# Feed-forward up-projection of a transformer block: eight column pairs by seven block products instead of five, and the low halves of the down-projection's operands added by memory queues

## The chip, the cores and the metric

The kernel runs on one core of a Trainium2 chip. The metric is the device time of one execution in microseconds (us), as the median of several. The engines are named as the profile names them: PE (matrix products; PEld loads its stationary operand), DVE (elementwise on vectors), ACT (elementwise functions and copies), POOL (here it issues transfers and does little else) and SP (issues most transfers).

## The reference, cut to what matters

The kernel computes one layer on a sequence of 512 tokens with 1024 features: a normalisation, one input projection, two attention branches, an output projection with a residual, and then a gated feed-forward block with a causal convolution of width 3. The change lies in the feed-forward block:

```
D_MODEL = 1024; SEQ = 512; D_FF = 2816
def conv_glu(x, w_up, conv_w, conv_b, w_down):
    hid = x @ w_up                                   # 512 x 1024 by 1024 x 5632
    hid = conv_general_dilated(hid, conv_w, padding=((2, 0),), feature_group_count=2 * D_FF) + conv_b
    gate, up = hid[..., :D_FF], hid[..., D_FF:]
    return (silu(gate) * up) @ w_down                # 512 x 2816 by 2816 x 1024
...
x = x + conv_glu(rms_norm(x, norm2_g), w_ffn_up, ffn_conv_w, ffn_conv_b, w_ffn_down)
```

All of it is in float32.

## The kernel before

**Products in three parts.** PE multiplies operands that were rounded to a shorter float32 form. To keep accuracy, each operand is split in a high half (the rounded value, by ACT) and a low half (value minus high half, by DVE), and each product is three matmuls: high by high, high by low, low by high.

**The up-projection** (22 column pairs, up0 to up21) takes 128 columns of the gate half and the 128 matching columns of the up half at a time. A plain pair (`up_body`) is 48 matmuls of 512 tokens. A pair whose number stands in the table `SEVEN` (line 63: 5, 8, 11, 14, 17) is computed in `up_seven` (line 986) as a 2 x 2 by 2 x 2 block product with seven block products in place of eight; it is 84 matmuls of 256 tokens. For it, sums of the weight's blocks (`block_sums`, line 173, tile `sx`) and of the activations' blocks (`token_sums`, tiles `ts`) are formed first, and `up_seven` adds the seven products up into `hg` and `hu` with further DVE and ACT steps. After either kind, ACT and DVE do the convolution (`conv`: one ACT step, two DVE steps, for gate and for up) and the gate; the result stands in one of the four slots of `ub`.

**The operands of the down-projection.** After every second pair, `pair_sums` (line 870) takes the two new slots of `ub` as one column pair: four DVE sums into `st` (one buffer) and in place, and then high and low halves of the seven operands into two tiles, `ax` and `ay` (`halves`: a cast on ACT and a subtraction on DVE, four times). For the first seven column pairs `ay` is stored in memory (`ayd`) and fetched back later (`fetch`, line 948).

**The weights** come in chunks of 1 MB into the tile `raw` (two buffers; `load`, line 113, issued by SP). While PE works on one pair, the next pair's chunk is split into `whi` and `wlo` (two buffers each) by `split_gen`, or `split_seven` for a pair of seven products, with further tiles `wxh` and `wxl` (one buffer each) for the block sums. A chunk's load is issued when the chunk two before it has been split.

**The down-projection** (`down_body`, chunks dn0_0 to dn0_10 and dn1_0 to dn1_10) is another seven-product scheme, over `ax` first and over `ay` second.

**What sets the order.** Engines run their own instructions in order. Program order gives each instruction a priority (`run_chunk`, line 242, interleaves a pair's matmuls with the split of the next), and a scheduler lays out each engine's order from that. So the order on an engine may differ from the order of the source. In `BANK` (line 773) the eight accumulators are dealt out in turns.

## Time and profile before

| | us |
|---|---|
| median of 3 runs | 725.97 (725.83 to 726.38) |
| the profiled execution, its own time | 726.66 |
| its span, first to last instruction | 724.9 |
| PE busy | 718.6 (99% of the span) |
| DVE busy | 565.4 (78%) |
| ACT busy | 401.5 (55%) |
| POOL busy | 53.6 (7%) |

In a line of the timeline the first number is the start in us from the span's start, the second the duration. In a line of groups the numbers behind the bar are the busy time, the mean duration in ns, and the idle time before. The up-projection runs from about 403 to 616 us, the down-projection from 616 us to the end.

### The profile page before, as it was taken

The page shows a single profiled execution, that of the slowest core. Times are in us where ns is not written, and L with a number is a line of the kernel's source. Part 1 is how long each engine was busy: PE and PEld are TensorE (multiplying, and loading weights), DVE is VectorE, ACT ScalarE, POOL GpSimd, SP SyncE. Part 2 cuts the span into 40 slices and gives each one's busy share as a digit, 9 for nine tenths or more (in the row PEclk, how much of TensorE's full clock was granted, in tenths as well). Part 3 has the DMA queues.
Part 4 walks back from the last instruction along what each step waited for, and adds up shares of the span by engine and source line. Part 5 has one row for each costly group of instructions (what it writes and reads, how often), then busy time and mean ns, then how long its engine had stood idle before and what let it go on. Part 6 is the DMA issues. An engine that isn't in the chain of part 4 may idle for free.

```text
span 724.9 us, 10589 instructions
## 1 busy us (share of the span) xinstructions
PE 718.6 (99%) x4019; PEld 627.5 (87%) x4019; DVE 565.4 (78%) x1030; ACT 401.5 (55%) x727; POOL 53.6 (7%) x95
## 2 busy tenths in 40 slices
PE   8999999999999999999999999999999999999997
PEld 8999998888988888888889889889898988888886
DVE  6678867775988888566275799998979985997686
ACT  6675656657767676442254556655545653543541
POOL 2701200000101011000012000000000100000000
PEclk9999999999999999999999999999999999999999
DMA  8632232211313111314536613544335553564563
GB/s 308 250 131 78 83 117 74 74 59 58 118 63 113 59 59 59 136 68 144 195 149 239 203 62 156 186 135 160 118 145 186 181 184 117 173 243 174 177 222 116
DMA packets 24786, 100.91 MB, mean 139 GB/s; under 512 B 2592, under 2 KB 7328, under 8 KB 17184
## 3 DMA queue, kind: packets, MB, share of 16 engines
q1 hardware_dynamic: 21792, 87.00, 33.8%
q0 software_dynamic: 2656, 13.11, 5.0%
q8 instruction: 31, 0.51, 0.3%
q14 instruction: 19, 0.16, 0.1%
q10 hardware_dynamic: 288, 0.14, 0.1%
HBM read 88.44 MB, written 11.80 MB: 138 GB/s over the span
## 4 chain that ended last, share of the span: by engine, by line
PE 98%; DMA 1%; SPq 0%; DVE 0%; ACT 0%; DVEq 0%; issue 0%
PE P L1087 14%; PE p L998 7%; PE pg L254 4%; PE pg L253 4%; PE pg L255 4%; PE pu L254 4%; PE pu L255 4%; PE pu L253 4%; PE qkB L255 2%; PE gB L255 2%; PE qkB L253 2%; PE gA L253 2%; PE gA L254 2%; PE gB L253 2%; PE gA L255 2%; PE qkB L254 2%
## 5 line engine op out<-in xcount | busy, mean ns | idle before, releaser
L253 PE MATMUL pg<-hth,whi_up 128*128 128x512 f32 (+1 forms) x152 | 55.7, 367 | 0.0
L255 PE MATMUL pg<-hth,wlo_up 128*128 128x512 f32 (+1 forms) x152 | 55.7, 366 | 0.0
L254 PE MATMUL pg<-htl,whi_up 128*128 128x512 f32 (+1 forms) x152 | 55.7, 366 | 0.0
L254 PE MATMUL pu<-htl,whi_up 128*128 128x512 f32 (+1 forms) x152 | 55.6, 366 | 0.0
L253 PE MATMUL pu<-hth,whi_up 128*128 128x512 f32 (+1 forms) x152 | 55.6, 366 | 0.0
L255 PE MATMUL pu<-hth,wlo_up 128*128 128x512 f32 (+1 forms) x152 | 55.6, 365 | 0.0
L1087 PE MATMUL P<-whi_dn,ax 128*128 128x512 f32 x176 | 54.4, 389 | 0.0
L149 ACT CAST whi_dn<-raw_dn 128x1024 fp32r<-128x1024 f32 x33 | 34.3, 1051 | 25.5 <-PE P L1087 15.2
L145 DVE TENSOR_TENSOR wlo_dn<-raw_dn,whi_dn 128x1024 fp32r<-128x1024 f32 x33 | 40.0, 1224 | 9.2 <-ACT whi_dn L149 9.1
L228 DVE TENSOR_TENSOR wlo_up<-raw_up,whi_up 128x1024 fp32r<-128x1024 f32 (+1 forms) x40 | 41.2, 1062 | 7.0 <-ACT whi_up L226 7.0
L226 ACT CAST whi_up<-raw_up 128x1024 fp32r<-128x1024 f32 (+1 forms) x40 | 34.5, 917 | 14.7 <-PE pu L254 7.9
L1087 PE MATMUL P<-whi_dn,ay 128*128 128x512 f32 x132 | 40.8, 389 | 0.0
L1087 PEld LDWEIGHTS P<-whi_dn,ax 128*128 128x128 f32 x176 | 33.0, 188 | 6.8
L1087 PE MATMUL P<-wlo_dn,ax 128*128 128x512 f32 x88 | 34.2, 389 | 0.0
L254 PEld LDWEIGHTS pu<-htl,whi_up 128*128 128x128 f32 x152 | 28.6, 188 | 4.7
L253 PEld LDWEIGHTS pu<-hth,whi_up 128*128 128x128 f32 x152 | 28.5, 188 | 4.7
L255 PEld LDWEIGHTS pg<-hth,wlo_up 128*128 128x128 f32 x152 | 28.6, 188 | 4.7
L255 PEld LDWEIGHTS pu<-hth,wlo_up 128*128 128x128 f32 x152 | 28.5, 188 | 4.6
L253 PEld LDWEIGHTS pg<-hth,whi_up 128*128 128x128 f32 x152 | 28.6, 188 | 4.6
L254 PEld LDWEIGHTS pg<-htl,whi_up 128*128 128x128 f32 x152 | 28.6, 188 | 4.5
L633 DVE TENSOR_TENSOR_SCAN aB<-aB,reset 128x127 f32<-128x127 f32 (+3 forms) x32 | 26.0, 817 | 6.7 <-ACT aB L628 6.7
L1087 PEld LDWEIGHTS P<-whi_dn,ay 128*128 128x128 f32 x132 | 24.8, 188 | 5.1
(303 smaller groups left out, 2240.3 us busy)
## 6 DMA issues: line engine op xcount, KB each, us to landing
raw_up<-in_wts SPq DMA_DIRECT2D x22, 1024.0 KB, 4.8
raw_dn<-in_wd SPq DMA_DIRECT2D x11, 1024.0 KB, 4.8
raw_dn<-in_wd SPq DMA_DIRECT2D x11, 512.0 KB, 3.4
ayd<-ay POOLq DMA_DIRECT2D x7, 768.0 KB, 5.2
ay<-ayd POOLq DMA_DIRECT2D x7, 768.0 KB, 6.5
raw_gA<-in_wts SPq DMA_DIRECT2D x4, 1024.0 KB, 4.7
raw_qkB<-in_wts SPq DMA_DIRECT2D x4, 1024.0 KB, 4.8
raw_gB<-in_wts SPq DMA_DIRECT2D x4, 1024.0 KB, 4.7
```

What stands on the lines that cost most here:

```text
L145: chain("halves", V.tensor_tensor(o, x, y, op=op))
L149: chain("casts", A.copy(hi[:, sl], src))
L226: A.copy(hi[:, sl], raw[:, sl])
L228: E.tensor_tensor(lo[:, sl], raw[:, sl], hi[:, sl].bitcast(F32), op=ALU.subtract)
L253: PE.matmul(ps, sh, mh, start=first, stop=False)
L254: PE.matmul(ps, sh, ml, start=False, stop=False)
L255: PE.matmul(ps, sl, mh, start=False, stop=last)
L633: V.tensor_tensor_scan(ar, ar, reset[:, S - n:S - 1][:, ::-1], 1.0, op0=ALU.mult, op1=ALU.max)
L998: PE.matmul(ps, st, mv[:, k, :], start=first and k == 0 and n == 0, stop=last and k == 3 and n == 2, skip_group_check=True)
L1087: chain("products", PE.matmul(dst, st, mv, start=first and n == 0, stop=last and n == 2, skip_group_check=True))
```

## The change

The table `SEVEN` becomes 5, 8, 10, 12, 14, 16, 18, 20: eight pairs in place of five, from 8 on every second one. With it go these edits:

- `halves`, for the first nine column pairs: the low half is no longer subtracted on DVE. ACT writes the negated, rounded value into the low half (one more ACT step), and a transfer issued by POOL adds the unrounded value to it in place. The same form is used for the ninth column pair, which had tiles of its own.
- `up_fin`: a column pair's steps (sums, `ax`, `ay`, the store) go into a list `todo`, from which `run_chunk` takes one at each yield of the following pairs. `ay` has two buffers now (the two staging tiles), and its store comes a column pair later in the program.
- `ax0` is stored too (`axd`) and fetched back later into a slot of `ts`.
- `block_sums` and `split_seven`: the block sums are formed in place in `raw`, with one tile `s1` left of `sx`; the four sums and five low halves become four sums and five low halves of other sizes (the 1024-wide one of `sx` becomes two of 512).
- `pc` shrinks to one block; the copies of `up_seven` go into parts of `hg` and `hu` that are still free.
- The fetches of `ay` move: one after the last pair of seven, the others between the chunks of the down-projection.

The diff, cut to its core:

```diff
-SEVEN = (5, 8, 11, 14, 17)
+SEVEN = (5, 8, 10, 12, 14, 16, 18, 20)
...
     def block_sums(i):
-        sx = late["pool"].tile([P, 1536], F32, tag="sx", name=f"sx_{order[i]}")
+        s1 = late["s1"] = late["pool"].tile([P, S], F32, tag="s1", name=f"s1_{order[i]}")
         V.tensor_tensor(s1, b[:, 1], b[:, 3], op=ALU.add)
         yield
-        V.tensor_tensor(s2, s1, b[:, 0], op=ALU.subtract)
-        yield
-        V.tensor_tensor(s4, b[:, 2], s2, op=ALU.subtract)
-        yield
         V.tensor_tensor(b[:, 1], b[:, 0], b[:, 1], op=ALU.subtract)
...
+        part(hi, lo, 0, raw[:, 0:1024])
+        V.tensor_tensor(b[:, 0], s1, b[:, 0], op=ALU.subtract)
+        yield
+        part(wh, wl, 0, s1)
+        part(wh, wl, 512, b[:, 0])
+        yield
+        part(hi, lo, 1024, raw[:, 1024:2048])
+        V.tensor_tensor(b[:, 2], b[:, 2], b[:, 0], op=ALU.subtract)
+        yield
+        part(wh, wl, 1024, b[:, 2])
...
         for _ in body(*splits.pop(key)):
             next(sp, None)
+            if late.get("todo"):
+                late["todo"].pop(0)()
             yield
...
-                ins.append(V.tensor_tensor(a[:, n + o:n + sl.stop], src, a[:, sl].bitcast(F32), op=ALU.subtract))
+                if i < 9:
+                    A.activation(lo, src, AF.Copy, scale=-1.0)
+                    G.dma_start(lo, src, accum_op=ALU.add)
+                else:
+                    ins.append(V.tensor_tensor(lo, src, a[:, sl].bitcast(F32), op=ALU.subtract))
...
-            for step in pair_sums(j // 2):
-                step()
-            if j // 2 < 7:
-                G.dma_start(ayd[j // 2], pairs[j // 2][1].bitcast(F32))
+            i = j // 2
+            late["todo"] += pair_sums(i)
+            if 0 < i < 8:
+                late["todo"].append(lambda: G.dma_start(ayd[i - 1], pairs[i - 1][1].bitcast(F32)))
+            if i == 6:
+                late["todo"].append(lambda: G.dma_start(axd, pairs[0][0].bitcast(F32)))
...
-        if j == 18:
-            for i in range(5):
-                fetch(i)
+        if j == SEVEN[-1]:
+            keep[0] = fp.tile([P, S], F32, tag="hg", name="t2_0")
+            ax0 = fp.tile([P, 2048], F32R, tag="ts", name="ax0_", bufs=4)
+            G.dma_start(ax0, axd)
+            pairs[0] = (ax0, None)
+            fetch(0)
...
+            n = ({1: 1, 3: 5, 5: 6, 7: 2, 9: 3}, {0: 4})[s].get(i)
+            if n is not None:
+                fetch(n)
```

The order on the engines up to the split of up5 is the same in both kernels. Three places of the rest are shown. The first is PE in the middle of a pair of seven products; p1 and p6 are accumulators of that pair, pg that of the next plain pair's gate. Before, up11:

```order
L998 MATMUL p6_11_5268<-ts2_4565,wxh_up11_5208 128x256 x2
L998 MATMUL p6_11_5268<-ts2_4565,wxl_up11_5209 128x256
L998 MATMUL p1_11_5265<-hth_99,whi_up11_5206 128x256
L998 MATMUL p1_11_5265<-htl_100,whi_up11_5206 128x256
L998 MATMUL p1_11_5265<-hth_99,wlo_up11_5207 128x256
```

The same place in the changed kernel, in up10:

```order
L1008 MATMUL p6_10_5209<-ts2_4569,wxh_up10_5143 128x256 x2
L1008 MATMUL p6_10_5209<-ts2_4569,wxl_up10_5144 128x256
L258 MATMUL pg11_5344<-hth_99,whi_up11_5226 128x512
L259 MATMUL pg11_5344<-htl_100,whi_up11_5226 128x512
L1008 MATMUL p1_10_5206<-hth_99,whi_up10_5141 128x256
```

Two matmuls of the next pair, up11, now stand between the fourth and the fifth product of up10 (and two of up17 in up16); in the kernel before, seven of up18 stood so in up17.

The second place is DVE around the start of a chunk's block sums. In the kernel before, the low halves of a column pair's `ay` and `ax` (L909) stand among them:

```order
L228 TENSOR_TENSOR wlo_up10_5119<-raw_up10_4965,whi_up10_5118 128x1024
L183 TENSOR_TENSOR sx_up11_5155<-raw_up11_5026,sx_up11_5155 128x512
L1024 TENSOR_TENSOR hu8_4993<-hu8_4993,pc8_4991 128x256
L228 TENSOR_TENSOR wlo_up10_5119<-raw_up10_4965,whi_up10_5118 128x1024
L909 TENSOR_TENSOR ay3_4972<-ub_4184,ay3_4972 128x256
L899 TENSOR_TENSOR ub_4184<-ub_4184 128x256
L900 TENSOR_TENSOR st3_4973<-st3_4973,ub_4184 128x256
L853 SCALAR_TENSOR_TENSOR cg8_5081<-hg8_4992,par_88,cg8_5081 128x511
L200 TENSOR_TENSOR wxl_up11_5209<-sx_up11_5155,wxh_up11_5208 128x1024
L909 TENSOR_TENSOR ax3_4971<-st3_4973,ax3_4971 128x256
```

In the changed kernel, from the last step that reads up10's `raw` (the first row) to the first that reads up12's (`s1_up12`) and a little further:

```order
L195 TENSOR_TENSOR wxl_up10_5144<-raw_up10_4981,wxh_up10_5143 128x512
L859 SCALAR_TENSOR_TENSOR cg9_5164<-pg9_5127,par_88,cg9_5164 128x511
L860 SCALAR_TENSOR_TENSOR cg9_5164<-pg9_5127,par_88,cg9_5164 128x510
L231 TENSOR_TENSOR wlo_up11_5227<-raw_up11_5033,whi_up11_5226 128x1024 x2
L859 SCALAR_TENSOR_TENSOR ub_4185<-pu9_5128,par_88,ub_4185 128x511
L177 TENSOR_TENSOR s1_up12_5272<-raw_up12_5198 128x512
L860 SCALAR_TENSOR_TENSOR ub_4185<-pu9_5128,par_88,ub_4185 128x510
L1020 TENSOR_TENSOR pc10_5210<-hu10_5212,pc10_5210 128x256
```

The rows of low halves of `ay` and `ax` are gone. Between the last use of one `raw` and the first use of the next chunk in the same buffer stand five DVE steps (the two of `wlo_up11` share a row), and behind that first use stand the steps that read up9's last accumulator and those of up10.

The third place is ACT at a pair of seven products. Before, at up11 (`pc` takes the copies of p1, p5 and p7):

```order
L851 ACTIVATE ub_4184<-pu10_5193,par_88 128x512
L908 CAST ax4_5174<-st4_5176 128x256
L908 CAST ay4_5175<-ub_4184 128x256
L908 CAST ax4_5174<-ub_4184 128x768
L1003 COPY pc11_5269<-p1_11_5265 128x256
```

In the changed kernel, at up10:

```order
L229 CAST whi_up11_5226<-raw_up11_5033 128x1024 x2
L857 ACTIVATE ub_4185<-pu9_5128,par_88 128x512
L873 ACTIVATE cg9_5164<-cg9_5164 128x512
L1013 COPY hg10_5211<-p1_10_5206 128x256
L1016 COPY hu10_5212<-p5_10_5207 128x256
L1019 COPY pc10_5210<-p7_10_5208 128x256
L1026 COPY hg10_5211<-p1_10_5206 128x256
L910 CAST ay4_5205<-ub_4185 128x256
L913 ACTIVATE ay4_5205<-ub_4185 128x256
```

The column pair's casts stand behind the copies of the seven products now, each with a negated copy (L913) at its side, and the first copy of p1 stands behind the gate step of the plain pair (cg9).

More of the change, by code (lines that the diff above doesn't have):

```diff
@@ L175, in block_sums @@
         b = raws[i].rearrange("p (b c) -> p b c", c=512)
-        sx = late["pool"].tile([P, 1536], F32, tag="sx", name=f"sx_{order[i]}")
-        late["sx"] = sx
-        s1, s2, s4 = (sx[:, 512 * j:512 * (j + 1)] for j in range(3))
+        s1 = late["s1"] = late["pool"].tile([P, S], F32, tag="s1", name=f"s1_{order[i]}")
         V.tensor_tensor(s1, b[:, 1], b[:, 3], op=ALU.add)
-        yield
-        V.tensor_tensor(s2, s1, b[:, 0], op=ALU.subtract)
-        yield
-        V.tensor_tensor(s4, b[:, 2], s2, op=ALU.subtract)
         yield
@@ L193, in split_seven, with part @@
         splits[key] = tuple(t.rearrange("p (k c) -> p k c", c=P) for t in (hi, lo, wh, wl))
-        sx = late["sx"]
-        for j, (h, l, src) in enumerate(((hi[:, 0:1024], lo[:, 0:1024], raw[:, 0:1024]),
-                                         (wh[:, 0:1024], wl[:, 0:1024], sx[:, 0:1024]),
-                                         (hi[:, 1024:2048], lo[:, 1024:2048], raw[:, 1024:2048]),
-                                         (wh[:, 1024:1536], wl[:, 1024:1536], sx[:, 1024:1536]))):
-            A.copy(h, src)
-            V.tensor_tensor(l, src, h.bitcast(F32), op=ALU.subtract)
-            if j < 3:
-                yield
+        b = raw.rearrange("p (b c) -> p b c", c=512)
+        s1 = late["s1"]
+        def part(h, l, c0, src):
+            sl = slice(c0, c0 + src.shape[-1])
+            A.copy(h[:, sl], src)
+            V.tensor_tensor(l[:, sl], src, h[:, sl].bitcast(F32), op=ALU.subtract)
+        part(hi, lo, 0, raw[:, 0:1024])
[8 more added lines that the diff above has]
+        part(wh, wl, 1024, b[:, 2])
     def split_gen(i, pieces):
@@ L265, in block_kernel @@
     ayd = dram.tile([7, P, 1536], F32, tag="ayd", name="ayd")
+    axd = dram.tile([P, 2048], F32, tag="axd", name="axd")
     reset = pool_c.tile([P, S], F32, tag="reset", name="reset")
@@ L875, in pair_sums @@
         t = {}
-        if i < 8:
+        if i < 9:
             ax = fp.tile([P, 2048], F32R, tag="ax", name=f"ax{i}", bufs=8)
-            ay = fp.tile([P, 1536], F32R, tag="ay", name=f"ay{i}")
-        elif i == 8:
-            ax = fp.tile([P, 2048], F32R, tag="ts", name=f"ax{i}", bufs=4)
-            ay = fp.tile([P, 1600], F32R, tag="wxh", name=f"ay{i}")[:, 0:1536]
-            keep[0] = fp.tile([P, S], F32, tag="hg", name="t2_0")
+            ay = fp.tile([P, 1536], F32R, tag="ay", name=f"ay{i}", bufs=2)
         else:
@@ L907, in halves @@
                 sl = slice(o, o + src.shape[-1])
+                lo = a[:, n + o:n + sl.stop]
                 A.copy(a[:, sl], src)
-                ins.append(V.tensor_tensor(a[:, n + o:n + sl.stop], src, a[:, sl].bitcast(F32), op=ALU.subtract))
+                if i < 9:
+                    A.activation(lo, src, AF.Copy, scale=-1.0)
+                    G.dma_start(lo, src, accum_op=ALU.add)
+                else:
+                    ins.append(V.tensor_tensor(lo, src, a[:, sl].bitcast(F32), op=ALU.subtract))
             return ins
@@ L948, in fetch @@
     def fetch(i):
-        tag = {0: "sx", 1: "wxl"}.get(i, "ts" if i < 5 else "ax")
-        n, bufs = {"sx": (1536, 1), "wxl": (1600, 1), "ts": (2048, 4), "ax": (2048, 8)}[tag]
+        tag = {0: "wxl", 1: "wxh"}.get(i, "ts" if i < 5 else "ax")
+        n, bufs = {"wxl": (1600, 1), "wxh": (1600, 1), "ts": (2048, 4), "ax": (2048, 8)}[tag]
         ay = fp.tile([P, n], F32R, tag=tag, name=f"ay{i}", bufs=bufs)[:, 0:1536]
@@ L989, in body @@
             left, right = slice(0, 256), slice(256, 512)
-            pc = fp.tile([P, 3, 256], F32, tag="pc", name=f"pc{j}")
+            pc = fp.tile([P, 256], F32, tag="pc", name=f"pc{j}")
             hg = fp.tile([P, S], F32, tag="hg", name=f"hg{j}")
@@ L1002, in body @@
             prod(b1, r, 0, B(0, left), last=False)
-            A.copy(pc[:, 0], b1)
+            A.copy(hg[:, right], b1)
             yield
             prod(b5, w, 0, ts[1], last=False)
-            A.copy(pc[:, 1], b5)
+            A.copy(hu[:, left], b5)
             yield
             prod(b7, r, 1, ts[3], last=False)
-            A.copy(pc[:, 2], b7)
-            V.tensor_tensor(pc[:, 1], pc[:, 1], pc[:, 2], op=ALU.add)
+            A.copy(pc, b7)
+            V.tensor_tensor(pc, hu[:, left], pc, op=ALU.add)
             yield
             prod(b6, w, 1, ts[2])
-            V.tensor_tensor(hu[:, right], b6, pc[:, 0], op=ALU.add)
+            V.tensor_tensor(hu[:, right], b6, hg[:, right], op=ALU.add)
             yield
@@ L1023, in body @@
             V.tensor_tensor(hu[:, left], b7, hu[:, right], op=ALU.add)
-            V.tensor_tensor(hu[:, right], hu[:, right], pc[:, 1], op=ALU.add)
+            V.tensor_tensor(hu[:, right], hu[:, right], pc, op=ALU.add)
             up_fin(j, None, hu, g)
@@ L1050, in block_kernel @@
     late["ts"] = token_sums()
+    late["todo"] = []
     for j in range(NF):
@@ L1054, in block_kernel @@
             pass
-        if j == 18:
-            for i in range(5):
-                fetch(i)
+        if j == NF - 1:
+            for step in late["todo"]:
+                step()
+            late["todo"] = []
+        if j == SEVEN[-1]:
[4 more added lines that the diff above has]
+            fetch(0)
     BLK = {1: 0, 2: 1, 5: 2, 7: 3, 3: 0, 4: 1, 6: 2}
@@ L1174, in steps0 @@
             yield from late_pair(ss[i][:2])
-            fetch(i - 4)
     def steps1():
```

## The prediction

> **What bounds the kernel now.** I read the page first, for the share of each engine and the chain that ended last.

> ```profile
> span 724.9 us, 10589 instructions
> ...
> PE 718.6 (99%) x4019; PEld 627.5 (87%) x4019; DVE 565.4 (78%) x1030; ACT 401.5 (55%) x727; POOL 53.6 (7%) x95
> ...
> PE 98%; DMA 1%; SPq 0%; DVE 0%; ACT 0%; DVEq 0%; issue 0%
> ```

> PE holds 98% of the chain. A busy PE can still be a PE that is fed late, so the next view is what PE waited for in the whole span.

> ```profile
> PE warm L301 <- DVE warm L298: 1.1, 1, 1.1
> PE qA L379 <- ACT whi_qA L226: 0.6, 1, 0.6
> PE qA L379 <- DVE whi_qA L224: 0.4, 1, 0.4
> ```

> All three waits lie at the start of the kernel. In the up-projection PE never waits, so its time there is the sum of its matmuls, and only fewer or shorter matmuls make it shorter. The chain in order of time prices them: up6 starts at 445.49 us, the pair of seven products up8 at 467.28, up9 at 477.17.

> ```profile
> 445.49 0.23 PE pg L253
> ...
> 467.28 9.89 PE p L998 x84
> 477.17 0.23 PE pg L253
> ```

> Two plain pairs take 467.28 - 445.49 = 21.79 us, 10.895 each. A pair of seven products takes 9.89. The difference is 1.005 us a pair. What could spoil it is DVE, so I read the busy time of each engine (PE, PEld, DVE, ACT, POOL) over two stretches of three pairs each, one of seven products and two plain:

> ```profile
> 477.17:508.85 31.68, 31.68 (x182) 27.92 (x181) 29.43 (x48) 18.41 (x30) 1.07 (x2) 1.00 0.35 125
> 508.85:540.53 31.68, 31.68 (x182) 27.92 (x181) 26.00 (x40) 17.25 (x26) 0.53 (x1) 1.00 0.41 149
> ```

> DVE is busy 29.43 and 26.00 of 31.68 us, 87% on average, with PE at full clock (1.00).

> **The change part by part.**

> *PE.* Three more pairs become pairs of seven: 3 x 1.005 = 3.0 us less. The two matmuls of a later pair that move into up10 and up16 cost nothing by themselves. Everything else must be hidden behind PE, in periods of one plain pair and one of seven: 10.895 + 9.89 = 20.785 us.

> *DVE.* Durations in this trace overlap by the tail of each instruction, so I cost a step by the distance between starts of neighbours that did not wait.

> ```profile
> 476.74 0.69 DVE L928 TENSOR_TENSOR ub<-cg,ub 128x512 f32<-128x512 f32 x1
> 477.34 0.68 DVE L181 TENSOR_TENSOR sx_up<-sx_up,raw_up 128x512 f32<-128x512 f32 x1
> ...
> 481.28 1.22 DVE L228 TENSOR_TENSOR wlo_up<-raw_up,whi_up 128x1024 fp32r<-128x1024 f32 x1
> 482.41 0.42 DVE L909 TENSOR_TENSOR ay<-ub,ay 128x256 fp32r<-128x256 f32 x1
> 482.75 0.42 DVE L899 TENSOR_TENSOR ub<-ub 128x256 f32<-128x256 f32 x1
> ...
> 487.15 0.95 DVE L909 TENSOR_TENSOR ax<-ub,ax 128x768 fp32r<-128x768 f32 x1
> 488.02 0.75 DVE L854 SCALAR_TENSOR_TENSOR cg<-hg,par,cg 128x510 f32<-128x510 f32 x1
> 488.68 0.75 DVE L854 SCALAR_TENSOR_TENSOR ub<-hu,par,ub 128x510 f32<-128x510 f32 x1
> ```

> So 512 columns cost 0.60, 1024 cost 1.13, 256 cost 0.34, 768 cost 0.87, and a convolution step 0.66 us. Four low halves leave DVE per column pair: 0.87 + 0.34 + 0.34 + 0.60 = 2.15 us. What stays in a period of the changed kernel: four 1024-wide low halves of weights, 4.52; nine 512-wide steps (four block sums, three low halves, two gate products), 5.40; nine 256-wide ones (five in the pair of seven, four sums of the column pair), 3.06; eight convolution steps, 5.28. That is 18.26 of 20.785 us, 88%. The load per time is what it was: the low halves that leave pay for the pairs of seven that come closer together.

> *ACT* takes the negated copies.

> ```profile
> 477.09 2.00 ACT L226 CAST whi_up<-raw_up 128x1024 fp32r<-128x1024 f32 x2 [1.40 <-PE p L998]
> 478.99 0.40 ACT L908 CAST ay<-ub 128x256 fp32r<-128x256 f32 x1
> 479.30 0.82 ACT L851 ACTIVATE cg<-hg,par 128x512 f32<-128x512 f32 x1
> 480.02 1.03 ACT L199 CAST wxh_up<-sx_up 128x1024 fp32r<-128x1024 f32 x1
> ...
> 483.20 0.84 ACT L908 CAST ax<-ub 128x768 fp32r<-128x768 f32 x1 [0.60 <-DVE ub L899]
> ```

> The four casts of a column pair cost about 0.31 + 0.31 + 0.84 + 0.5 (512 columns, between the other two) = 2.0 us, and their negated copies as much again. By the windows ACT was busy 35.7 of 63.4 us, 56%; with 2.0 us and the denser pairs of seven I get about 70%. ACT has room.

> *Order within a period.* I laid the rows of the changed order out with these costs, from the start of a pair of seven such as up10 as time 0 (all of this is estimated from the rows above). At 0 PE has left up9, the buffer of `whi` is free, and ACT casts `whi_up11` until 2.0; DVE follows with `wlo_up11` until 3.4 and reaches `s1_up12` at 4.0. PE wants `whi_up11` at 4 x 12 x 0.1177 = 5.65 (9.89 us over 84 matmuls is 0.1177), because two matmuls of up11 stand there: 3.6 us in hand. The second accumulator of up9 is read by 5.2 and wanted after 9.89. The casts of up12 wait until PE has left up10; their first half is split by 14.5, and wanted at 20.785: 6.3 us in hand. The last step that reads up12's `raw` ends at 19.9; up14's load is issued then, and DVE wants it at 20.785 + 4.0 = 24.8. That leaves 4.9 us for a load:

> ```profile
> DMA to landing us min/median/max: 4.6/4.8/8.8
> ```

> Those are the loads of `raw_up`: 4.8 at the median just fits, and a late one delays `s1`. Behind `s1` on DVE stand the step that frees up9's second accumulator, and all steps of the pair of seven. A delay is not at once PE's: the first copy of p1 on ACT stands behind the gate step of the plain pair, which DVE feeds at 0.6, and PE writes p1 again at 5.65; DVE may be about 4.0 us late before PE waits. And DVE catches up as long as its loop is shorter than 20.785: from `s1` to the end of that chunk's last low half it has 14.0 us of work and 0.9 of waiting for ACT, then the load, then 0.2 for the handing over, 19.9 in all with 4.8. The loop breaks even at a load of 5.7 us.

> *Memory queues.* The trace of before shows no adding transfer. A column pair adds 1792 columns of 128 rows, 896 KB, in four transfers, issued by my layout from 8 to 13 us into the pair of seven. Three views bound them: the fetches at their busiest, then a load beside a store, then the stores and fetches by themselves.

> ```profile
> GB/s 195 66 186 213 252 326 405 441 423 354 177 9 0 0 0 0 0 159 239 425 310 0 20 86 246 412 425 425 430 405 396 418 403 427 399 47 13 9 133 337
> ...
> ay<-ayd POOLq DMA_DIRECT2D x5, 768.0 KB, 6.5
> raw_up<-in_wts SPq DMA_DIRECT2D x3, 1024.0 KB, 7.0
> ```

> ```profile
> raw_up<-in_wts SPq DMA_DIRECT2D x1, 1024.0 KB, 5.2
> ayd<-ay POOLq DMA_DIRECT2D x1, 768.0 KB, 5.4
> ```

> ```profile
> L933 POOL DMA_DIRECT2D ayd<-ay x7: 533/533/542, 438.8 to 553.9; - x7
> ...
> DMA to landing us min/median/max: 3.5/5.3/9.0
> ```

> At 425 GB/s the adds hold the queues for 2.2 us of a period; two loads hold them for 4.9 and the store for 1.9. Landing lies between 3.5 (the fastest store) and 18 us (twice the slowest, for a slow adder); I take 5.3, the median, since the pieces are smaller than the store. Adds that land by 18 and a store that lands by 24 lie beside the start of the load at 19.9; a load beside one store took 5.2. The adds' own results are wanted late: `st` is written again at 28, the `ub` slot at 35. POOL issues five transfers of 0.53 us a period and has nothing else to do, so their cost there is nothing; without that cover it would be 2.7 us a period.

> [...]

> *The way into the down-projection.* `ax0` returns by POOL as soon as PE has left the second product of up20, some 18 us before PE wants it; the fetches beside it took up to 9.0. Its cost is nothing; if it came at twice 9.0, nothing still. The other fetches, moved into the down-projection, are wanted a whole first pass later (264 matmuls of 0.23, some 60 us).

> *The sum.* The profiled execution took 726.66 us, 1.8 more than its span and 0.7 more than the median. Less 3.0 it is 723.6, and against the median 725.97 - 3.0 = 723.0.

> **The rivals.**

> *Loads too slow for the loop (slower).* If the loads of `raw` reach 7.0 us beside the adds and the store, as three did beside the fetches, the loop is 22.1 us, 1.3 over the period. Five loops from up10 to up20 lose 6.5, of which 4.0 are hidden: 2.5 us, a net of 725.5. Up to 6.8 the loss stays at 5 x 1.1 - 4.0 = 1.5 and within the forecast's side. From 7.4 us on the kernel is slower than before by over 1.45: 5 x 1.7 - 4.0 = 4.5 lost against 3.0 won. At 8.8, the slowest seen, 5 x 3.1 - 4.0 = 11.5, and the time is 734.5. For it speaks that the load just fits; against it, that a load beside one store took 5.2 and that the adds fall between the loads. PE would wait for ACT's copy of p1, or for `whi`.

> *The adds themselves too slow (slower).* `st` has one buffer; the next column pair's sums wait for the adds, and DVE stands behind them. From those sums to the last add's issue are 5.7 us, so the loop is 5.7 plus the landing, and breaks even at a landing of 15. At 18 it is 23.7, 2.9 over; seven more column pairs lose 20.4, less 4.0 hidden: 16.4, and the time is 739.4. The nearest rows (3.5 to 9.0) speak against it.

> *The change gains half.* A single slow load now and then, or the down-projection's first chunk late by a microsecond or two, costs 1.6 to 4.4 us once: 724.6 to 727.4.

> **How the numbers follow.** A measurement of this kernel can tell about 0.2%, 1.45 us, from no change. The forecast has 0.62: every term that must be hidden has a margin by the rows, except the load. The middle case has 0.13, loads over 7.4 have 0.18, and slow adds have 0.07. So faster is 0.62, the same 0.13, slower 0.25. At the low end nothing can give more than the three pairs; with the spread of the runs, 0.5 us, that is 722.4. At the high end the range takes in the middle case and loads up to 7.7 us (5 x 2.0 - 4.0 = 6.0 lost), 729.0; what it leaves out is 0.17.

> **What would show it.** Right: the pairs of seven at 9.89 us and the plain ones at 10.9, up21 ending 3.0 us earlier, no wait of PE in the up-projection, DVE at about 88% there, loads of `raw_up` at about 5. The first rival would show as waits of DVE's `s1` step for `raw_up`, and of PE for ACT's copies into `hg` or for `whi`; the second as waits for `st` or `ub` on a transfer from POOL. The prediction is wrong if PE waits between up8 and dn0_0 for more than 1.5 us in sum, or if the plain pairs stretch without a wait in the trace.

## The result, and the profile after

The changed kernel takes 732.97 us (median of 4 runs, 731.74 to 734.34), the kernel before 725.90 (4 runs, 725.54 to 726.38): a ratio of 1.0097, 95% interval 1.0084 to 1.0109. It is slower by 7.1 us; the forecast was 3.0 faster. The profiled execution took 733.51 us with a span of 731.5, 6.6 more than the span before.

The page of the changed kernel: span, engines, the queue that POOL feeds (packets, MB, share of 16 engines), and the chain that ended last.

```profile
span 731.5 us, 11010 instructions
...
PE 718.2 (98%) x4127; PEld 629.9 (86%) x4127; DVE 567.3 (78%) x1035; ACT 426.7 (58%) x789; POOL 86.3 (12%) x133
...
q0 software_dynamic: 8128, 23.47, 12.3%
...
PE 82%; DVE 5%; DMA 5%; issue 4%; ACT 2%; POOL 1%; SPq 0%; DVEq 0%; POOLq 0%; ACTq 0%
```

PE's share of the chain fell from 98% to 82%; DVE, the memory queues and POOL, which held 1% of it or less, hold 5, 5 and 1% now. PE's busy time didn't change (718.2 us, 718.6 before), although three more pairs are of the kind that is 1.0 us shorter: part of it is matmuls at a lower clock (0.84 in the mean of the 11 us around the stop in up8, below). What PE waited for, over the whole span (us in total, times, longest):

```profile
PE p L1008 <- ACT hg L1013: 2.9, 1, 2.9
PE qA L385 <- ACT whi_qA L229: 2.4, 1, 2.4
PE P L1105 <- DVE wlo_dn L145: 1.2, 2, 0.8
...
PE p L1008 <- DVE wlo_up L195: 0.8, 1, 0.8
PE p L1008 <- ACT whi_up L194: 0.4, 1, 0.4
```

Three waits on L1008, 4.1 us, are all in one pair of seven products; two on L1105 are in the first pass of the down-projection; that on `qA` is at the start of the kernel. Three pieces of the chain in order of time show that one pair (start, length) beside others:

```profile
478.09 5.97 PE p L1008 x36
...
501.09 4.09 PE p L1008 x36
515.63 9.89 PE p L1008 x84
```

The second part of up8, 36 matmuls, took 5.97 us where the same 36 of up10 took 4.09. PE had stood still for 2.90 us ahead of it and ran at a mean clock of 0.84 in these 11 us (clock, share of the DMA engines and GB/s are the last three columns):

```profile
474.00:485.00 11.00, 8.10 (x51) 7.73 (x51) 10.44 (x19) 7.47 (x15) 2.83 (x4) 0.84 0.92 277
```

From the first matmul of up5 to the first of up9 it is 47.9 us (436.0 to 483.9), before 41.6: 6.3 us lost in up8, of which 4.1 are waits and 5.97 - 4.09 = 1.9 the lower clock (0.50 granted from 478.92 to 482.12 us). The rest, 0.3, is by estimate the overlap of neighbouring matmuls that each stop breaks (rows of 0.28 us start 0.11 apart). From up9 to the first matmul of `P` it is 135.4 us, before 138.6: the 3.2 us that the forecast hoped for. From the first to the last matmul of `P` it is 107.5 us, before 104.7: 2.8 lost. The start of the kernel came 0.6 later. Together 0.6 + 6.3 - 3.2 + 2.8 = 6.5 of the 6.6 us.

**Why up8 stalls.** DVE ahead of it waits 6.61 us for a transfer before it may write `st`:

```profile
457.32 0.69 DVE L935 TENSOR_TENSOR ub<-cg,ub 128x512 f32<-128x512 f32 x1
464.62 0.42 DVE L899 TENSOR_TENSOR st<-ub 128x256 f32<-128x256 f32 x1 [6.61 <-DMA ay<-st]
```

That transfer is the last add of the column pair before. POOL's rows at that place (in brackets: how long POOL did nothing, and what it is put down to):

```profile
444.49 0.56 POOL L940 DMA_DIRECT2D ayd<-ay  x1 [6.51 <-DVE st L899]
449.00 0.89 POOL L914 DMA_DIRECT2D ay<-ub  x1 [3.95 <-DVE hu L1034]
452.44 0.86 POOL L914 DMA_DIRECT2D ax<-st  x1 [2.55 <-ACT ub L857]
455.44 0.84 POOL L914 DMA_DIRECT2D ax<-ub  x1 [2.15 <-DVE ub L859]
461.22 0.86 POOL L914 DMA_DIRECT2D ay<-st  x1 [4.93 <-issue]
```

The four adds (L914) don't go out together. They land 3.1, 2.7, 5.5 and 3.3 us after their issue, at 452.1, 455.1, 460.9 and 464.5, and each of the other three starts 0.3 us after the landing of the one above, whatever DVE or ACT row the trace puts the gap down to. The first of them went out 0.3 us after the store of `ax0` had landed (at 448.7), 5.1 us behind the sums. So 15.5 us pass from the first issue to the last landing, while `st` of the next column pair is wanted at 458.0.

**The way into the down-projection.** The chain holds two loads of `raw_dn` there:

```profile
619.52 8.66 DMA raw_dn<-in_wd
...
638.49 7.14 DMA raw_dn<-in_wd
```

The landing (min/median/max) of all 22 loads of `raw_dn` in the kernel before:

```profile
DMA to landing us min/median/max: 3.0/4.4/4.9
```

The same in the changed kernel:

```profile
DMA to landing us min/median/max: 3.2/4.3/10.3
```

The slow ones were issued between 602 and 644 us, when `ax0` and five fetches of `ay` came back (POOL issued them from 601.88 to 616.28; they took 6.2 to 11.7 us), and then the last two fetches (636.73 and 642.60).

### The profile page after: what moved, and what is told of

It reads as the page before. It is cut to its first block, busy times and chain, and to the rows that moved or that the text cites. A ratio compares the mean times of both kernels' runs of the same rounds, so it can differ in the third digit from the quotient of the medians.

```text
span 731.5 us, 11010 instructions
## 1 busy us (share of the span) xinstructions
PE 718.2 (98%) x4127; PEld 629.9 (86%) x4127; DVE 567.3 (78%) x1035; ACT 426.7 (58%) x789; POOL 86.3 (12%) x133
## 4 chain that ended last, share of the span: by engine, by line
PE 82%; DVE 5%; DMA 5%; issue 4%; ACT 2%; POOL 1%; SPq 0%; DVEq 0%; POOLq 0%; ACTq 0%
PE P L1105 10%; PE p L1008 9%; DMA raw_dn<-in_wd 2%; PE pg L258 2%; PE pu L258 2%; PE pg L260 2%; PE pg L259 2%; PE pu L259 2%; PE pu L260 2%; PE qkB L260 2%; PE gB L260 2%; PE qkB L258 2%; PE gA L259 2%; PE gB L258 2%; PE gA L258 2%
## 5 line engine op out<-in xcount | busy, mean ns | idle before, releaser
L1105 PE MATMUL P<-whi_dn,ax 128*128 128x512 f32 x160 | 49.5, 390 | 0.0
L258 PE MATMUL pg<-hth,whi_up 128*128 128x512 f32 (+1 forms) x128 | 46.4, 363 | 0.0
L260 PE MATMUL pg<-hth,wlo_up 128*128 128x512 f32 (+1 forms) x128 | 46.4, 362 | 0.0
L259 PE MATMUL pg<-htl,whi_up 128*128 128x512 f32 (+1 forms) x128 | 46.3, 362 | 0.0
L259 PE MATMUL pu<-htl,whi_up 128*128 128x512 f32 (+1 forms) x128 | 46.3, 362 | 0.0
L258 PE MATMUL pu<-hth,whi_up 128*128 128x512 f32 (+1 forms) x128 | 46.3, 362 | 0.0
L260 PE MATMUL pu<-hth,wlo_up 128*128 128x512 f32 (+1 forms) x128 | 46.2, 361 | 0.0
L1105 PE MATMUL P<-whi_dn,ay 128*128 128x512 f32 x132 | 40.8, 389 | 0.0
L231 DVE TENSOR_TENSOR wlo_up<-raw_up,whi_up 128x1024 fp32r<-128x1024 f32 (+1 forms) x34 | 33.6, 1032 | 5.6 <-ACT whi_up L229 5.4
L229 ACT CAST whi_up<-raw_up 128x1024 fp32r<-128x1024 f32 (+1 forms) x34 | 28.5, 894 | 12.8 <-PE pu L259 9.1
L1105 PEld LDWEIGHTS P<-whi_dn,ax 128*128 128x128 f32 x160 | 30.0, 188 | 6.1
L1105 PE MATMUL P<-wlo_dn,ax 128*128 128x512 f32 x80 | 31.7, 396 | 1.5 <-DVE wlo_dn L145 1.2
L641 POOL TENSOR_SCALAR_AFFINE_SELECT bB<-bB 128x128 f32<-128x128 f32 x32 | 13.7, 430 | 149.1 <-DVE bB L640 139.5
L1105 PEld LDWEIGHTS P<-whi_dn,ay 128*128 128x128 f32 x132 | 24.8, 188 | 5.1
L670 ACT CAST pth_A<-pT_A 128x128 fp32r<-128x128 f32 (+2 forms) x40 | 14.7, 371 | 22.4 <-PE pT_A L657 14.7
## 6 DMA issues: line engine op xcount, KB each, us to landing
raw_up<-in_wts SPq DMA_DIRECT2D x22, 1024.0 KB, 5.7
raw_dn<-in_wd SPq DMA_DIRECT2D x11, 1024.0 KB, 5.8
ayd<-ay POOLq DMA_DIRECT2D x7, 768.0 KB, 5.7
ay<-ayd POOLq DMA_DIRECT2D x7, 768.0 KB, 9.1
raw_gA<-in_wts SPq DMA_DIRECT2D x4, 1024.0 KB, 4.8
raw_qkB<-in_wts SPq DMA_DIRECT2D x4, 1024.0 KB, 4.8
raw_gB<-in_wts SPq DMA_DIRECT2D x4, 1024.0 KB, 4.8
```

The costliest lines, as they stand in the source:

```text
L229: A.copy(hi[:, sl], raw[:, sl])
L231: E.tensor_tensor(lo[:, sl], raw[:, sl], hi[:, sl].bitcast(F32), op=ALU.subtract)
L258: PE.matmul(ps, sh, mh, start=first, stop=False)
L259: PE.matmul(ps, sh, ml, start=False, stop=False)
L260: PE.matmul(ps, sl, mh, start=False, stop=last)
L641: G.affine_select(b[:, n - P:n], b[:, n - P:n], pattern=[[-1, P]], compare_op=ALU.is_gt, fill=0.0, base=0, channel_multiplier=1)
```

## The experiments

The theories, as the expectations number them. First: what sends the adds out one after the other is the room that transfers issued by POOL are given (`dynamic_dma_scratch_size`, 512 bytes in both kernels). The expectations take it for memory that holds descriptors; the runs show it only by how many transfers are on their way. Its rivals: something that more room wouldn't mend, such as the adds' own speed and traffic (2); the store of `ax0` that stands among the adds in POOL's queue (3). Fourth, for the down-projection's part: the fetches that moved there slow its loads. The kernel before took 726.06 to 726.22 us beside these runs.

### More room

```diff
-    nc = bacc.Bacc("TRN2", target_bir_lowering=False, num_devices=1, dynamic_dma_scratch_size=512)
+    nc = bacc.Bacc("TRN2", target_bir_lowering=False, num_devices=1, dynamic_dma_scratch_size=1024)
```

> The changed kernel with twice the memory for descriptors of POOL's transfers (1024 bytes a partition in place of 512); the order on every engine is the same. Theory 1 (descriptor room): an add fills so much of that room that POOL can't issue the next before the last has landed; with twice the room the adds of a column pair go out about 0.9 us apart, the last lands some 8 us earlier, the 6.6 us wait of the sums step for the adds is gone and with it PE's loss of 6.4 us in up8: 733.0 - 6.4 = 726.6 us. Theory 2 (the adds themselves are slow, in the queues): the adds issue earlier but each lands later, the last one lands when it did, up8 still loses about 6 us: 732 to 734 us. Both leave the 2.8 us that are lost at the start of the down-projection.

Measured: 724.89 us (10 runs, 724.64 to 726.73), ratio 0.9990 (0.9981 to 0.9999), 8.1 us less than the change with the same instructions in the same order on every engine. POOL's rows for the adds of the column pair ahead of up8:

```profile
458.20 0.84 POOL L914 DMA_DIRECT2D ay<-ub  x1 [3.68 <-DVE ub L900]
459.48 0.87 POOL L914 DMA_DIRECT2D ax<-st  x1 [0.44 <-DVE cg L859]
460.95 0.86 POOL L914 DMA_DIRECT2D ax<-ub  x1 [0.59 <-ACT ax L913]
464.58 0.84 POOL L914 DMA_DIRECT2D ay<-st  x1 [2.76 <-ACT ay L913]
```

All that PE waited for in this kernel, at its start:

```profile
PE qA L385 <- ACT whi_qA L229: 1.3, 1, 1.3
PE warm L307 <- DVE warm L304: 1.1, 1, 1.1
```

The first three adds went out before the first landed (at 461.7, 3.5 us after its issue), and the last landed 9.7 us after the first issue. Three is the most here: of the column pair before, the fourth add went out at 450.04, 0.3 us after the first had landed, with the second and third still on their way. The landing (min/median/max) of all adds in the changed kernel:

```profile
DMA to landing us min/median/max: 2.6/3.9/7.3
```

And with 1024 bytes, where it is nearly the same, so that it is not the speed of one add that made the difference:

```profile
DMA to landing us min/median/max: 2.6/3.5/6.5
```

DVE waits for no add, PE for nothing in the up-projection; up5 to up9 takes 41.6 us as before the change. The first theory holds, and the second falls.

### Room between the two

The same line with 768 in place of 1024.

> The changed kernel with 768 bytes for POOL's descriptors. If 512 bytes hold three plain transfers, an add counts as two of them, and the room grows with the bytes, 768 hold four: two adds are on their way at a time, and only the third waits for the first to land. A column pair's four adds then end some 5 us sooner than with 512 bytes, the wait of 6.6 us for st falls under 2 us and PE's loss in up8 goes; the fetches at the way into the down-projection go out four at a time: 725 to 728 us. Rival: the room comes in coarser steps (768 works as 512): adds one after the other as in the change, 731 to 734 us.

Measured: 725.17 us (10 runs, 724.43 to 726.92), ratio 0.9991 (0.9981 to 1.0001). POOL's rows for one column pair:

```profile
443.02 0.86 POOL L914 DMA_DIRECT2D ay<-ub  x1 [5.76 <-DVE hu L1023]
443.69 1.07 POOL L914 DMA_DIRECT2D ax<-st  x1
450.09 0.84 POOL L914 DMA_DIRECT2D ax<-ub  x1 [5.33 <-ACT cg L857]
450.77 1.03 POOL L914 DMA_DIRECT2D ay<-st  x1
```

Two adds go out at once; the third follows 0.3 us after the first has landed (449.8), the fourth 0.3 after the second (450.5). So the number of adds on their way is 1, 2 and 3 with 512, 768 and 1024 bytes, and two are enough: PE waits for nothing in the up-projection here, and 0.4 us at the down-projection. Of plain transfers five were on their way at the fetches, one more than expected, and the sixth went out 0.3 us after the first had landed; with 512 bytes it is three, as the kernel before had shown already, in rows that I hadn't read this way (the three of the first row land from 578.0 on):

```profile
572.82 1.61 POOL L953 DMA_DIRECT2D ay<-ayd  x3 [18.37 <-PE p L998]
578.29 0.54 POOL L953 DMA_DIRECT2D ay<-ayd  x1 [3.86 <-PE pg L255]
```

### The store moved behind the adds

```diff
-                    G.dma_start(lo, src, accum_op=ALU.add)
+                    late["add"] = (G.dma_start(lo, src, accum_op=ALU.add),)
...
-                late["todo"].append(lambda: G.dma_start(axd, pairs[0][0].bitcast(F32)))
+                late["todo"].append(lambda: behind(G.dma_start(axd, pairs[0][0].bitcast(F32)), late["add"]))
```

> The changed kernel with the store of the first column pair's ax moved from right behind its adds to behind the adds of the seventh column pair. Theory 3 (place of this store): it holds the descriptor room and the queues from 437 to 449 us, so that the second column pair's adds start 5 us late; without it they end some 5 to 7 us earlier, the sums step waits 0 to 2 us instead of 6.6, and the time is 726.6 to 728 us. Theory 1 in its strict form (adds one after the other are enough to lose the time) gives 731 to 733: the four adds of a column pair still take 15 us.

Measured: 731.68 us (4 runs, 729.62 to 735.05), ratio 1.0081 (1.0052 to 1.0110). The adds of the second column pair still went out from 447.4 to 463 us, one after the other, and DVE waited for them at five places:

```profile
DVE st L899 <- DMA ay<-st: 16.6, 5, 7.5
```

The four started 1.1 us behind their sums in place of 5.1, as theory 3 had it, but the last landed 20.2 us behind them, 20.6 in the change: the landings themselves took longer (5.2, 2.6, 7.1 and 3.2 us), and they still stand in a row. Theory 3 falls as the cause; what the store's place is worth, at most the 1.3 us between the medians, is inside the spread of these four runs.

### The fetches issued by SP

```diff
-                SP.dma_start(raw, wd0[n])
+                late["ld"] = (SP.dma_start(raw, wd0[n]),)
...
-        G.dma_start(ay, ayd[i])
+        if i == 0:
+            G.dma_start(ay, ayd[i])
+        else:
+            behind(SP.dma_start(ay.bitcast(F32), ayd[i]), late["ld"])
```

> The changed kernel with six of the seven fetches of ay issued by SP, each behind a weight load of the down-projection, in place of POOL just after the last pair of seven. Theory 4 (the fetches slow the weight loads): raw_dn loads land in 5 to 6 us, in place of up to 10, PE does not wait at the start of the down-projection, 2.8 us come back: 730.2 us. Rival (DVE comes late out of the up-projection, and the loads only look late): PE still waits for the split of dn0 chunks, 732 to 734 us. The loss in up8 stays with both.

Measured: 731.61 us (730.78 to 732.62), ratio 1.0072 (1.0055 to 1.0088). All of PE's waits behind the start:

```profile
PE p L1011 <- ACT whi_up L194: 1.9, 1, 1.9
...
PE p L1011 <- ACT hg L1016: 1.5, 1, 1.5
PE p L1011 <- DVE wlo_up L195: 0.8, 1, 0.8
```

The waits on L1105 are gone and the down-projection's matmuls take 104.8 us again, 2.7 less than in the change; the loss in up8 (L1011 here) stays. That is the fourth theory by the trace. The medians are 1.4 us apart, but four runs each overlap (731.74 to 734.34 in the change), so they alone don't show it. The loads didn't come down to the 5 to 6 us that were expected: some of `raw_dn` still take up to 9.3, but none of them is late for PE.

### The low halves on DVE

```diff
-                if i < 9:
+                if i < 0:
```

All eight pairs of seven, no add: every low half is subtracted on DVE again.

> Eight pairs of seven products, but all low halves subtracted on DVE as before, no adds by transfers. By the ledger DVE has 18.3 + 2.15 = 20.4 us of work in a period of 20.8 us. If DVE is then the bound (theory 5: the adds are needed), DVE falls behind by its waits for ACT and for loads, about 1 us a period, and PE loses 2 to 6 us by up20: 725 to 730 us. If the slack of the buffers is enough (rival: the adds were not needed for eight pairs), PE loses nothing in the up-projection, only the fetches cost some 2 us: 723 to 725 us.

Measured: 727.44 us (6 runs, 726.88 to 729.37), ratio 1.0023 (1.0011 to 1.0035). The up-projection has one wait of 0.3 us; among the first matmuls of `P`, 4.6 us in, PE waits for DVE's last convolution steps:

```profile
PE P L1105 <- DVE cg L860: 1.1, 1, 1.1
PE p L1008 <- ACT pc L1019: 0.3, 1, 0.3
```

From up5 to `P` it is 178.0 us, 2.2 less than before; the matmuls of `P` take 106.8 us in place of 104.7, 2.1 more. So without the adds the three pairs give back at the way into the down-projection what they bring. 1.1 of that is the wait for DVE; the rest lies beside loads of `raw_dn` of up to 9.5 us, and may be the fetches'. The time is in the range of theory 5, but not where it had the loss: by the start of `P` PE was only 1.0 us behind the kernel with adds and 1024 bytes (177.0). That the median is slower than before by 1.4 us also holds a start that came 1.0 later in this profile.

### Five pairs of seven with the adds

```diff
-SEVEN = (5, 8, 10, 12, 14, 16, 18, 20)
+SEVEN = (5, 8, 11, 14, 17)
```

> The changed kernel with the old table (five pairs of seven products) and everything else of the change. Theory 1: the loss comes from the adds of the second column pair in the third one's way, before the tables differ, so up8 loses about 6 us here too, and the start of the down-projection up to 3: 726.0 + 6 + 0 to 3 = 732 to 735 us. Rival (the closer pairs of seven overload DVE): no loss with five, 726 to 727 us.

Measured: 740.90 us (4 runs, 740.55 to 741.47), ratio 1.0204 (1.0190 to 1.0218): slower than with eight pairs, and by more than I expected of any theory. What DVE waited for at `st`:

```profile
DVE st L899 <- DMA ay<-st: 19.4, 6, 8.9
```

And PE's three longest waits:

```profile
PE P L1105 <- DVE ub L860: 4.1, 2, 3.8
PE p L1008 <- ACT whi_up L194: 2.9, 1, 2.9
PE p L1008 <- ACT hg L1013: 1.4, 1, 1.4
```

DVE waits for the adds six times. Up8 loses again, and here DVE also comes late to the last column pairs, so that PE waits at the start of the down-projection.

> Five sevens with the adds and all else of the change, as in the run that took 740.9 us, with 1024 bytes for POOL's descriptors in place of 512; the order of every engine is the same. If the whole loss of that run is adds that go one after the other, it goes: no wait of st for an add, no wait of PE in the up-projection, and the time is that of the changed kernel with 1024 bytes (724.89) plus what the three pairs of seven give, up to 3.0: 726 to 728 us, the kernel before within 0.3%. Rival: the old table puts the column pairs' steps beside the wrong steps of DVE and ACT, whatever the adds do: 730 us or more, with PE waiting for ub at the start of the down-projection (4.1 us there with 512 bytes).

The same kernel with 1024 bytes: 726.05 us (10 runs, 725.65 to 726.78), ratio 0.9995 (0.9986 to 1.0005). DVE waits for no add, PE for nothing but the start. All 14.9 us were the room. And the adds themselves, with room, cost nothing that can be measured: five pairs with subtractions take the same (725.98 with this room, below).

### Adds from the third column pair on

```diff
-                if i < 9:
+                if 1 < i < 9:
```

The first two column pairs' low halves are subtracted on DVE; 512 bytes.

> The changed kernel with the low halves of the first two column pairs subtracted on DVE, and adds from the third on, with the old 512 bytes of descriptor memory. Theory 1: adds one after the other (15 us a column pair) do harm only where two column pairs follow each other within 15 us, as the second and third do; from then on they are 20.8 us apart. So up8 loses nothing or little (0 to 1 us) and the time is 726 to 728 us. Rival (adds in a row also cost in the later periods, hidden behind the early loss): 729 to 733.

Measured: 732.22 us (4 runs, 730.36 to 733.76), ratio 1.0083 (1.0066 to 1.0100). Up8 takes 9.89 us now, but PE waits in up10 and up12:

```profile
495.48 0.39 PE L1008 MATMUL p<-hth,whi_up 128*128 128x256 f32 x1 [1.48 <-ACT hg L1013]
518.52 0.39 PE L1008 MATMUL p<-hth,whi_up 128*128 128x256 f32 x1 [2.11 <-ACT hg L1013]
```

DVE waits 9.8 us for adds at three places. That only the first column pairs are too close together is wrong: with the adds beginning two column pairs later, the column pairs behind them still run into them.

### Room alone, and the best version

The kernel before with 1024 bytes:

> The kernel before with 1024 bytes of descriptor memory; the order on every engine is the same. Theory 1: its stores and fetches never made PE wait, so the time is the same, 726.0. Rival (the room for descriptors is a gain of its own, and the 724.9 is partly that): 724.5 to 725.5. Its profile also shows whether the first loads of the kernel, which landed 1 to 2 us later in the profiles since, do so without the change as well.

Measured: 725.98 us (10 runs, 725.50 to 726.50), ratio 0.9998 (0.9989 to 1.0008): without adds the room is worth nothing. The changed kernel with 1024 bytes and with the fetches on SP:

> The changed kernel with 1024 bytes of descriptor memory and with six fetches of ay issued by SP behind the weight loads. Theories 1 and 4 together: the first alone gave 724.9; its profile still showed one late split at the start of the down-projection and its last matmul 0.5 us later against the first of the down-projection than in the kernel before, so 0.5 us more come back: 724.4 us. Rival (the fetches cost nothing once the adds are fast): 724.9.

Measured: 724.77 us (11 runs, 724.04 to 726.32), ratio 0.9984 (0.9976 to 0.9993), faster than both kernels, by 0.2% of the kernel before; it can't be told from 1024 bytes alone (724.89). The medians side by side:

| | 512 bytes | 1024 bytes |
|---|---|---|
| five pairs, subtractions (the kernel before) | 726.1 | 725.98 |
| five pairs, adds | 740.90 | 726.05 |
| eight pairs, subtractions | 727.44 | not tried |
| eight pairs, adds (the change) | 732.97 | 724.89 |

## Why the prediction was wrong

**PE: three pairs, 3.0 us.** Right where nothing stalls: 138.6 - 135.4 = 3.2 us from up9 on, and with 1024 bytes 177.0 us from up5 to `P` against 180.2 before, 3.2 again.

**DVE at 88%, ACT with room, the order within a period.** They held: from up9 to up21 PE waited for nothing in the changed kernel, with loads of `raw_up` at 5.7 us in the median (single ones up to 10.2), just where my loop breaks even. Over two periods from the start of up12 (515.63 to 557.23 us) DVE was busy 92%, somewhat more than the forecast, and ACT 72%. The rival of slow loads didn't decide.

**Memory queues.** This is the step that failed: "POOL issues five transfers of 0.53 us a period and has nothing else to do, so their cost there is nothing", with four adds issued "from 8 to 13 us into the pair of seven" and one landing of 5.3 behind them. That put at nothing what the issue of one transfer waits for in the transfers before it. The landing was no worse than I took it (3.9 in the median). But POOL sent the next add only when the one before had landed, so that four landings stand in a row: from the sums ahead of up8's wait (443.9 us) to the last landing (464.5) it is 20.6 us in place of 5.7 + 3.9 = 9.6; with 1024 bytes it is 11.3 (442.3 to 453.6). I asked of the rows only how long one transfer takes, not how many can be on their way. The place was off too: my loop could be 20.8 us long, since I took the sums to be so far apart, but those of the first column pairs come 15 us apart (with 1024 bytes L899 starts at 427.3, 442.3, 457.1, 476.8 and 497.9 us), so it was up8 that lost 6.3 us. The rival of adds too slow named the wait, for `st` with DVE behind it, but not its cause, and had a chance of 0.07; its sign came (6.6 us for `st`), and so did the prediction's own sign of being wrong, with 4.1 us of PE's waits in place of at most 1.5. The rival's time, 739.4, assumed a loss in all later column pairs, and only the first one or two cost PE time; my reading is that the time lost there itself moves the later sums away from the adds.

**The speed of an add.** No run shows the landing of 18 us that the forecast allowed for a slow adder: in the change an add landed after 2.6 to 7.3 us, and the slowest of all these runs after 10.1 (five pairs, 1024 bytes), in a kernel whose DVE waited for no add. With room for three, the same adds at nearly the same landing (3.5 us in the median, 3.9 with 512 bytes) cost PE nothing.

**The way into the down-projection.** "Its cost is nothing" was wrong by a smaller amount: the fetches went out at the end of the up-projection and not a pass later, beside the loads of the first chunks, and these took up to 5.4 us longer than the 4.9 of before. With the fetches held back behind the loads, 2.7 us came back in the profile.

**What stays open.** The three pairs are worth 3.2 us in the up-projection, but 726.05 - 724.89 = 1.2 in the medians with 1024 bytes. In the two profiles the spans are 2.1 us apart (724.7 and 722.6): half a microsecond is in the matmuls of `P` (105.2 us from first to last, 104.7 before), and half lies ahead of the up-projection, which began at 378.8 and 379.3 us. The time outside the span takes another 0.3 (a run is some 1.75 us longer than its span with five pairs, 2.05 with eight and adds), and the remaining 0.6 is that the two profiled executions lie further apart than the medians. Over all profiles the up-projection began between 378.1 and 381.6 us, the kernel before with 378.9 among them (the 403 us given ahead of the prediction is the start of up2, not of up0); what sets that I didn't try. Why up10 and up12 lose less than up8 when the adds begin with the third column pair isn't settled either.

## What to carry to other kernels

Work moved to transfers that POOL issues was priced here by how many of them could be on their way (one, two and three adds with 512, 768 and 1024 bytes: 732.97, 725.17 and 724.89 us), not by the landing of one (3.9, 3.8 and 3.5 us in the median): look in the profile for issues that start 0.3 us after an earlier landing, and try the size of that room by itself before the rest of the change is judged. A chain of small transfers behind one buffer (15.5 us here from the first issue to the last landing) has to be compared with the smallest distance between two users of that buffer (15 us), and not with the mean period (20.8). A move of fetches that "aren't wanted yet" is a move of traffic beside loads that are: loads of `raw_dn` took up to 10.3 us here, 4.9 before.

## What the runs showed of the hardware

**The clock after a short stop.** The rows of PE's matmuls of 256 columns around the stop in up8 of the changed kernel:

```profile
474.92 0.28 PE L1008 MATMUL p<-ts,wxl_up 128*128 128x256 f32 x1
478.09 0.39 PE L1008 MATMUL p<-hth,whi_up 128*128 128x256 f32 x1 [2.90 <-ACT hg L1013]
...
478.67 0.28 PE L1008 MATMUL p<-htl,whi_up 128*128 128x256 f32 x1
478.78 0.34 PE L1008 MATMUL p<-hth,wlo_up 128*128 128x256 f32 x1
478.92 0.42 PE L1008 MATMUL p<-hth,whi_up 128*128 128x256 f32 x1
479.13 0.41 PE L1008 MATMUL p<-htl,whi_up 128*128 128x256 f32 x1
...
482.12 0.35 PE L1008 MATMUL p<-hth,wxh_up 128*128 128x256 f32 x1
482.31 0.28 PE L1008 MATMUL p<-htl,wxh_up 128*128 128x256 f32 x1
482.43 0.28 PE L1008 MATMUL p<-hth,wxl_up 128*128 128x256 f32 x1
```

They start 0.11 us apart at first, then 0.21 from 478.92 to 482.12, then 0.12 again, and the granted clock was 0.50 in these 3.2 us, 0.96 in the 0.8 ahead of them and in the 1.9 behind: the stop of 2.9 us cost up to 1.9 more behind it, most of it at half the speed for 3.2 us. The kernel with adds from the third column pair on narrows it down: its stop of 2.11 us in up12 is followed by 3.4 us at half the speed (starts 0.21 apart from 519.10 to 522.51), its stop of 1.48 in up10 by none. So a stop of 2.1 us was enough here and one of 1.5 wasn't, and the longer one cost nearly twice its length (up12 took 3.9 us more than its 9.8 from first to last start).
